# Four heads per tile, unnormalised weights and a ones column in the mixer of a two-block network

## The chip, the cores and the metric

The program runs on one core of a Trainium2 chip. The metric is device time in microseconds (us) of one execution; before the change three runs took 1721.58, 1722.12 and 1723.14 us, with a median of 1722.12. The core has a matrix engine (PE, with its weight loads as PEld), a vector engine (DVE), an activation engine (ACT), GpSimd (POOL) and a queue of loads (SP). Each works through its own list of instructions in order and waits on semaphores for the others.

## The reference, cut to what matters

Two blocks run one after the other on 256 tokens of width 1024. The second block has two layers, and each holds one mixer, the part that is changed. Cut to it:

```python
def hybrid_mixer(h, ...):
    z = h @ w_in
    q_lat, kv_lat, k_rope, qkv_d = jnp.split(z, [c0, c1, c2], axis=-1)
    q = (rmsnorm_2(q_lat, q_norm) @ w_q_up).reshape(B, S, 8, 64 + 32)
    kv = (rmsnorm_2(kv_lat, kv_norm) @ w_kv_up).reshape(B, S, 8, 64 + 64)
    ...
    o_mla = mla_attention(q_nope, q_rope, k_nope, k_rope, v_mla)   # 8 heads, causal
    qd, kd, vd = [t.reshape(B, S, 8, 64) for t in jnp.split(qkv_d, 3, axis=-1)]
    qd, kd = apply_rope(qd, cos_d, sin_d), apply_rope(kd, cos_d, sin_d)
    o_dil = dilated_attention(qd, kd, vd).reshape(B, S, 512)       # 8 heads, dilated windows
    merged = concatenate([rmsnorm_2(o_mla, gain[:512]), rmsnorm_2(o_dil, gain[512:])])
    return merged @ w_out

def apply_rope(x, cos, sin):
    x1, x2 = jnp.split(x, 2, axis=-1)
    return jnp.concatenate([x1 * cos - x2 * sin, x2 * cos + x1 * sin], axis=-1)
```

The kernel turns the three dilated windows into one masked softmax (the mask tile holds the logarithm of how often a key is seen), so both kinds of heads are a softmax of 256 queries over 256 keys, of which the first 128 queries see 128 keys.

## The kernel before, in words

Weights stream from memory in chunks of 16 blocks of 128x128. ACT copies half a chunk into a tile `whi` in a rounded format, DVE writes the rest, raw minus `whi`, into `wlo`, and PE multiplies with three matmuls a block (`whi` with both parts of the activations, `wlo` with one). These matmuls, called dense here, have 256 or 512 moving columns. The softmax parts use plain fp32, where one matmul leaves two records in the trace.

A recording layer (`Recorder`, L374) takes all operations of the program, gives each a due time, and puts each engine's list in the order of a modelled start (`order`, L472). PE takes what can start first, so softmax matmuls stand between dense ones that come later in the source. PSUM has eight tiles called `bank`; scratch tiles are called `n`, small columns `sm`, and the tiles of one stage `part`.

The mixer (L1634) streams these stages: `vd` (values of the dilated heads), `za` and `zb` (six tiles of 128 columns of z each), `kn`, `vm` and `q` (keys, values and queries of the other heads), and `o` (the product with w_out). Heads of the dilated kind (i = 1) start while `zb` streams, those of the other kind (i = 0) while `q` streams. `pipeline` (L1558) advances each live head by one step per new head.

- A tile of z has two heads of 64 rows. `rotate` (L1658) copies the four groups of 32 rows in swapped order with four ACT copies and then needs three DVE operations.
- One head's `attention` (L1449) is: a score matmul for the first 128 queries and one for the other 128; on DVE a masked minimum (a custom operation), on ACT the exponential with its sum as a second output; then on DVE a reciprocal and two divisions, on PE three transposes, on ACT a copy, and `weighted` (L1477) multiplies values, held as weights of 64 columns, with the transposed softmax.

```python
            nc.scalar.activation(s[:, a], s[:, a], AF.Exp, scale=-1.0, bias=m[:, t:t + 1], accum_out=den[:, t:t + 1])
        rd = self.small(2)
        nc.vector.reciprocal(rd, den)
        for t, a in enumerate((slice(0, P), slice(P, 384))):
            nc.vector.tensor_scalar(s[:, a], s[:, a], rd[:, t:t + 1], None, op0=OP.mult)
```

- Outputs have features on partitions, two heads in a bank. The norm of a kind (L1711 to L1723) squares on ACT, adds on DVE, sums over partitions on PE with `ones`, takes the power -0.5 on POOL, broadcasts with transposes of `sm` and multiplies on DVE.

In the trace nearly all of these operations carry one line, L667, where the recorded calls are made, so they are told apart by tiles.

## Time and profile before

| | |
|---|---|
| median of three runs | 1722.12 us |
| the profiled execution's own time | 1721.75 us |
| its span, first to last instruction | 1720.0 us |
| PE busy | 1669.3 us, 97% |
| DVE busy | 1198.2 us, 70% |
| ACT busy | 908.1 us, 53% |
| POOL busy | 59.5 us, 3% |

Matmuls are pipelined, so a record lasts longer than the time until the next one starts; what a matmul costs is read as the distance between starts. The first mixer lies at about 840 to 963 us, the second at about 1372 to 1494 us.

### The profile page before, as it was taken

Reading aid. Unit: us, or ns where it says so; the run is one execution under the profiler, and the core shown is the slowest. Engines: PE = TensorE matmul, PEld = TensorE weight load, DVE = VectorE, ACT = ScalarE, POOL = GpSimd, SP = SyncE. Lnnn points to the kernel's source line nnn. Section 1 sums busy time; section 2 is a strip of 40 time slices with the busy share of each in tenths; the row PEclk is TensorE's granted clock in tenths of the full one; section 3 lists DMA queues with packets and bytes.
Section 4 is the critical chain, followed back from the end, with each engine's and each line's share of the span. In section 5 each row is a group of like instructions: output and inputs, shape, how many; then the busy total and the mean of one; then the engine's idle time right before and its main releaser. Section 6 shows DMA issues by size and latency. Waiting matters only on the chain.

```text
span 1720.0 us, 22162 instructions
## 1 busy us (share of the span) xinstructions
PE 1669.3 (97%) x8452; PEld 1362.7 (79%) x8452; DVE 1198.2 (70%) x1992; ACT 908.1 (53%) x1451; POOL 59.5 (3%) x81
## 2 busy tenths in 40 slices
PE   7999999999999999999999999999999999999998
PEld 4777888879788887888887788887888887788886
DVE  4889999897786557664677756558665578766547
ACT  2784444446454435454577544456444468554435
POOL 0000000000000001000000100001000000000001
PEclk9999999999999999999999999999999999999999
DMA  8766999864375545554432545546455432364542
GB/s 337 262 253 269 344 349 350 327 229 188 135 296 178 189 172 212 186 195 178 181 132 74 189 174 194 183 173 217 177 193 185 158 148 99 128 233 178 190 171 86
DMA packets 49803, 348.81 MB, mean 203 GB/s; under 512 B 5765, under 2 KB 5901, under 8 KB 8480
## 3 DMA queue, kind: packets, MB, share of 16 engines
q1 hardware_dynamic: 46960, 338.73, 53.6%
q0 software_dynamic: 2304, 7.41, 1.3%
q8 instruction: 66, 1.08, 0.2%
q10 hardware_dynamic: 432, 1.26, 0.2%
q14 instruction: 41, 0.34, 0.1%
HBM read 346.31 MB, written 1.06 MB: 202 GB/s over the span
## 4 chain that ended last, share of the span: by engine, by line
PE 81%; DVE 9%; ACT 6%; issue 2%; DMA 1%; POOL 1%; POOLq 0%; ACTq 0%; DVEq 0%
PE bank L667 81%; DVE n L667 3%; ACT n L667 3%; DVE wlo L667 3%; ACT whi L667 2%; POOL sm L667 1%; DVE part L667 1%; DVE x L667 1%; DMA x<-in_x_dram 1%; ACT part L667 1%; DVE xhl L667 1%; DVE raw L667 0%; DMA raw<-in_wm_dram 0%; DVE sm L667 0%; ACT L667 0%
## 5 line engine op out<-in xcount | busy, mean ns | idle before, releaser
L667 DVE TENSOR_TENSOR wlo<-raw,whi 128x1024 fp32r<-128x1024 f32 (+1 forms) x575 | 651.0, 1144 | 372.4 <-ACT whi L667 371.1
L667 ACT ACTIVATE whi<-raw 128x1024 fp32r<-128x1024 f32 (+1 forms) x575 | 564.1, 993 | 504.0 <-PE bank L667 461.9
L667 PE MATMUL bank<-whi,xhl 128*128 128x512 f32 x2240 | 714.0, 395 | 6.3 <-ACT xhl L667 4.1
L667 PEld LDWEIGHTS bank<-whi,xhl 128*128 128x128 f32 x2240 | 419.3, 188 | 101.9 <-ACT xhl L667 9.2
L667 PE MATMUL bank<-whi,part 128*128 128x512 f32 x1464 | 462.8, 394 | 0.1
L667 PE MATMUL bank<-wlo,xhl 128*128 128x512 f32 x1120 | 439.5, 393 | 3.2 <-DVE wlo L667 2.7
L667 PEld LDWEIGHTS bank<-whi,part 128*128 128x128 f32 x1464 | 273.4, 188 | 59.1 <-DVE part L667 1.8
L667 PE MATMUL bank<-wlo,part 128*128 128x512 f32 x732 | 286.0, 391 | 0.0
L667 PEld LDWEIGHTS bank<-wlo,xhl 128*128 128x128 f32 x1120 | 210.6, 188 | 49.9 <-DVE wlo L667 8.2
L667 PEld LDWEIGHTS bank<-wlo,part 128*128 128x128 f32 x732 | 137.6, 188 | 29.0 <-issue 1.2
L667 PE MATMUL bank<-xhl,whi 128*128 128x256 f32 x768 | 146.9, 290 | 1.7 <-ACT xhl L667 1.6
L667 PEld LDWEIGHTS bank<-xhl,whi 128*128 128x128 f32 x768 | 121.6, 193 | 12.7 <-issue 6.7
L667 ACT ACTIVATE n<-bank 32x256 f32<-32x256 f32 (+3 forms) x172 | 80.2, 468 | 92.4 <-PE bank L667 85.9
L667 PE MATMUL bank<-xhl,wlo 128*128 128x256 f32 x384 | 109.3, 288 | 2.0 <-ACT part L667 2.0
L667 PE MATMUL bank<-ident,n 128*128 128x128 f32 x480 | 80.8, 278 | 14.2 <-DVE n L667 10.1
L667 POOL TENSOR_TENSOR sm<-sm,mhalf 128x1 f32<-128x1 f32 (+2 forms) x48 | 43.2, 904 | 1459.2 <-DVE sm L667 1386.0
L667 PEld LDWEIGHTS bank<-ident,n 128*128 128x128 f32 x480 | 59.0, 142 | 37.3 <-DVE n L667 12.2
L667 ACT ACTIVATE part<-bank 128x512 fp32r<-128x512 f32 (+3 forms) x112 | 55.8, 505 | 46.0 <-PE bank L667 44.3
L667 PEld LDWEIGHTS bank<-xhl,wlo 128*128 128x128 f32 x384 | 73.8, 192 | 4.7 <-ACT part L667 2.6
L667 DVE TENSOR_TENSOR part<-bank,part 128x512 fp32r<-128x512 f32 (+3 forms) x122 | 65.7, 551 | 3.6 <-ACT n L667 2.6
L667 ACT ACTIVATE n<-x 128x512 f32<-128x512 f32 x52 | 32.5, 625 | 58.2 <-DVE x L667 52.5
L667 DVE CUSTOM_DVE_ANT_0 raw<-raw,macc 128x1024 f32<-128x1024 f32 x48 | 57.5, 1222 | 3.5 <-DMA raw<-in_wm_dram 3.4
(141 smaller groups left out, 1152.7 us busy)
## 6 DMA issues: line engine op xcount, KB each, us to landing
raw<-in_ws_dram SPq DMA_DIRECT2D x266, 1024.0 KB, 4.8
raw<-in_wm_dram SPq DMA_DIRECT2D x56, 1024.0 KB, 6.2
macc<-in_rows_dram POOLq DMA_DIRECT2D x10, 512.0 KB, 5.2
x<-in_x_dram ACTq DMA_DIRECT2D x2, 512.0 KB, 12.3
n<-scr POOLq DMA_DIRECT2D x8, 128.0 KB, 6.8
out_dram<-x SPq DMA_DIRECT2D x4, 256.0 KB
n<-in_pt_dram POOLq DMA_DIRECT2D x4, 128.0 KB, 4.4
masks<-in_masks_dram POOLq DMA_DIRECT2D x1, 256.0 KB, 5.0
```

Of the source, the lines that this page charges most:

```text
L667: getattr(getattr(rec.nc, name), method)(*[real(v) for v in args], **{k: real(v) for k, v in kw.items()})
```

## The change

Six places differ. The columns of z are put in another order, so that a tile holds the first or the second 32 dimensions of four heads; the rotation is then two products and a difference or sum per tile, without ACT copies. Scores of the dilated kind are computed for four heads at a time from 32-row slices of these tiles, in two halves that add up in PSUM. `attend` takes two heads at once; the exponential gives no sum and nothing is divided before the transposes. The values have 65 columns a head, the last of them ones, and are now the moving operand, with the transposed softmax as weights, so the output has queries on partitions and the sum of the softmax in its 65th column. A reciprocal and one product on DVE then divide. The norm of a kind works on tiles with tokens on partitions (square with a sum on ACT, power on POOL, one product on DVE) and turns them with four transposes each before `o`. Between two stages a head step is skipped where the stream yields None.

The diff, cut; removed lines of the mixer stand in the listing above.

```diff
 def z_cols(u):
-    if u < 2:
-        return span(u)
-    if u == 2:
+    if u in (4, 5):
+        return span(u - 4)
+    if u == 10:
         return slice(256, 384)
-    if u == 3:
+    if u == 11:
         return KR_COLS
-    u -= 4
-    base = C2 + (u % 2) * 512 + (u // 2) * P
-    return slice(base, base + P)
+    g, i = divmod(u, 6)
+    return np.concatenate([C2 + (i // 2) * 512 + h * 64 + (i % 2) * 32 + np.arange(32) for h in range(4 * g, 4 * g + 4)])
...
+    def attend(self, ps, v, bias, scale, om):
+        nc = self.nc
+        s = []
+        for p in ps:
+            e, m = self.wide(384), self.small(2)
+            for t, a in enumerate((slice(0, P), slice(P, 384))):
+                nc.vector.tensor_tensor_reduce(e[:, a], p[:, a], bias[t], -scale, 1e38, op0=OP.add, op1=OP.min,
+                                               accum_out=m[:, t:t + 1])
+                nc.scalar.activation(e[:, a], e[:, a], AF.Exp, scale=-1.0, bias=m[:, t:t + 1])
+            s.append(e)
+        self.pe += 0.7
+        yield
+        w = []
+        for e in s:
+            pt = self.bank()
+            for i in range(3):
+                nc.tensor.transpose(pt[:, i * P:(i + 1) * P], e[:, i * P:(i + 1) * P], self.ident)
+            w.append(self.wide(384))
+            nc.scalar.activation(w[-1], pt[:, :384], AF.Copy)
+        self.pe += 0.7
+        yield
+        po = self.bank()[:, :260].split(65)
+        first = None
+        for t, parts in enumerate(((0,), (1, 2))):
+            for i in range(2):
+                for j in parts:
+                    o = nc.tensor.matmul(po[:, 2 * t + i], w[i][:, j * P:(j + 1) * P], v(j // 2, i), start=(t + i == 0),
+                                         stop=(j == parts[-1]), skip_group_check=True, after=first)
+                    first = first or o
+        rd = self.small(4)[:, :, None]
+        nc.vector.reciprocal(rd, po[:, :, 64:])
+        nc.vector.tensor_mul(om.flat().split(64), po[:, :, :64], rd.to_broadcast([P, 4, 64]))
+        self.pe += 0.7
     def mixer(self, l, h):
         nc = self.nc
         self.epoch()
         tl = self.tl
         rope, qlh, qd, kd = tl([3, T]), tl([3, 2 * T], FR), tl([4, T]), tl([4, T])
...
+        vd, vm, ka, qa = tl([2, 8, 65]), tl([2, 8, 65]), tl([8, T]), tl([8, T])
+        kr, lt, lr, oh = tl([T]), tl([T]), tl([512]), Halved(tl([2, 2, D], FR))
         accq, acck = self.squares(2), self.squares(1)
...
+        low, om = {}, {}
         rcol = self.r
...
+        for v in (vd, vm):
+            for t in range(2):
+                nc.vector.memset(v[:, t, :, 64:], 1.0)
+        def ropes():
+            pb = self.bank()
+            for t in range(2):
+                nc.tensor.transpose(pb[:, t * P:(t + 1) * P], rcol[t].to_broadcast([P, P]), self.ident)
+            r = nc.slot("rb", [P, T], FT)
+            nc.scalar.activation(r, pb[:, :T], AF.Copy)
+            for i, t in enumerate((self.cos_d, self.sin_d, self.rot_m)):
+                nc.vector.tensor_mul(rope[:, i], t, r)
+            return r
+        def rotate(da, db, pa, pb):
+            for dst, x, y, op in ((da, pa, pb, OP.subtract), (db, pb, pa, OP.add)):
+                t = self.tmp()
+                nc.vector.tensor_mul(t, y, rope[:, 1])
+                nc.vector.tensor_mul(dst, x, rope[:, 0])
+                nc.vector.tensor_tensor(dst, dst, t, op=op)
         half = slice(64, P)
+        held = {}
         def z(u, ps):
...
+            if not held:
+                held["r"] = ropes()
+            if u == 11:
                 nc.vector.tensor_mul(kr[half], ps[half, :T], rope[half, 2])
                 sw = self.tmp()
...
+                for i, j in ((64, 96), (96, 64)):
                     nc.scalar.activation(sw[i:i + 32], kr[j:j + 32], AF.Copy)
                 nc.vector.tensor_add(kr[half], kr[half], sw[half])
                 nc.vector.tensor_copy(ka[half], kr[half, None, :].to_broadcast([64, 8, T]))
...
+                return
+            g, i = divmod(u, 6)
+            if i < 4:
+                if i % 2 == 0:
+                    held[i] = ps
+                else:
+                    dst = (qd, kd)[i // 2]
+                    rotate(dst[:, 2 * g], dst[:, 2 * g + 1], held[i - 1], ps)
+                return
+            n = 2 if g else i - 4
+            ql = self.tmp()
+            nc.vector.tensor_mul(ql, ps[:, :T], held["r"])
+            acck[1](0, ql) if n == 2 else accq[1](n, ql)
+            self.hilo_scaled(qlh[:, n], ql, self.vec("kvn", l) if n == 2 else self.vec("qn", 2 * l + n))
+            if n == 2:
+                low["c"], _ = self.rnorm([(accq[0], 1.0 / 256), (acck[0], 1.0 / 128)], lr)
+                nc.vector.tensor_mul(lt, self.rot_m, lr[:, :T])
+        left = {}
+        def scores(i, j):
             if i == 0:
...
+                out = []
+                for u in (2 * j, 2 * j + 1):
+                    ps = self.bank()
+                    nc.tensor.matmul(ps[:, :P], qa[:, u, :P], ka[:, u, :P], start=True, stop=True)
+                    nc.tensor.matmul(ps[:, P:384], qa[:, u, P:], ka[:, u], start=True, stop=True)
+                    out.append(ps)
+                return out
+            if j % 2 == 0:
+                four = [self.bank() for _ in range(4)]
+                last = {}
+                for a, n in ((slice(0, P), P), (slice(P, 384), T)):
+                    for part in range(2):
+                        for e, ps in enumerate(four):
+                            b = slice(32 * e, 32 * e + 32)
+                            q, k = qd[b, j + part], kd[b, j + part]
+                            last[e] = nc.tensor.matmul(ps[:, a], q[:, a.start:a.start + P], k[:, :n], start=(part == 0),
+                                                       stop=(part == 1), share=4, after=last.get(e))
+                left[0] = four[2:]
+                return four[:2]
+            return left.pop(0)
+        def heads(i, j):
+            v = vd if i else vm
+            b, sc = (self.masks[:, :T], 64 ** -0.5) if i else (self.masks[:, T:], 96 ** -0.5)
+            if j == 0:
+                om[i] = self.row().split(T).split_last(P)
+            yield from self.attend(scores(i, j), lambda s, e: v[:, s, 2 * j + e], (b[:, P:], b), sc, om[i][:, j])
+            if j == 3:
+                for t in range(2):
+                    o, ss, m, r = om[i][:, :, t], self.small(1), self.small(1), self.small(1)
+                    nc.scalar.activation(self.wide().split(P), o, AF.Square, accum_out=ss)
+                    nc.vector.tensor_scalar(m, ss, 1.0 / 512, EPS, op0=OP.mult, op1=OP.add)
+                    nc.gpsimd.tensor_tensor(r, m, self.mhalf[:, :1], op=OP.pow)
+                    y = self.wide()
+                    nc.vector.tensor_scalar(y.split(P), o, r, None, op0=OP.mult)
+                    self.later(3.0, lambda t=t, y=y: self.turned(t, y, [(oh, self.vec("go", l * 8, 8), None)], 4 * i),
+                               oh.mem, t, range(4 * i, 4 * i + 4))
         def q_up(u, ps):
             nc.vector.tensor_mul(qa[:, u], ps[:, :T], lt)
@@ -1730,30 +1792,29 @@
                 a = slice(64 * s, 64 * s + 64)
                 nc.vector.tensor_mul(ka[:64, 2 * u + s], ps[a, :T], lr[a, T:])
+        def values(dst, scale):
+            return lambda t, _, ps: nc.scalar.activation(dst[:, t, :, :64], ps.split(64), AF.Copy, scale=scale(t))
         def stream():
...
+            self.natural(f"b{l}vd", h, values(vd, lambda t: rcol[t]), tail=None)
             self.units(f"b{l}za", h, z)
             yield heads(1, 0)
...
             for u in self.steps(f"b{l}zb", h, lambda u, ps: z(u + 6, ps)):
...
+                yield {0: 1, 3: 2, 4: 3}.get(u) and heads(1, {0: 1, 3: 2, 4: 3}[u])
             ql = Tall(qlh)
             for _ in self.steps(f"b{l}kn", ql, k_up, lambda k, u: 2):
                 pass
...
+            yield None
+            self.natural(f"b{l}vm", ql, values(vm, lambda t: low["c"][:, 2 + t:3 + t]), at=lambda k: 2)
             for u in self.steps(f"b{l}q", ql, q_up):
...
+                if u % 2:
+                    yield heads(0, u // 2)
         self.pipeline(stream())
         grow = self.fixed_row(l * 4 + 1)
         hn = self.xhl()
         then = self.gained([(hn, self.gain(l, 4), None)])
...
+        self.natural(f"b{l}o", oh, self.add_normed(grow, 1.0 / D, then), halves=2, tail=self.TAIL,
                      at=lambda k: (k + 4) % 8)
         return hn
```

On PE, the first scores of the first mixer; `xhl` is the mixer's input, `part_3` and `part_2` hold keys and queries. Before:

```order
L667 MATMUL bank_135<-xhl_77,whi_69 128x256 x2
L667 MATMUL bank_129<-part_3_5985,part_2_5984 128x128
L667 MATMUL bank_129<-part_3_5985,part_2_5984 128x256
L667 MATMUL bank_133<-part_3_5985,part_2_5984 128x128
L667 MATMUL bank_133<-part_3_5985,part_2_5984 128x256
L667 MATMUL bank_135<-xhl_77,wlo_74 128x256
```

The same place now:

```order
L676 MATMUL bank_131<-part_3_5975,part_2_5974 128x128
L676 MATMUL bank_135<-xhl_77,whi_70 128x256
L676 MATMUL bank_135<-xhl_77,wlo_75 128x256
L676 MATMUL bank_135<-xhl_77,whi_70 128x256 x2
L676 MATMUL bank_136<-part_3_5975,part_2_5974 128x128
L676 MATMUL bank_129<-part_3_5975,part_2_5974 128x128
L676 MATMUL bank_133<-part_3_5975,part_2_5974 128x128
L676 MATMUL bank_131<-part_3_5975,part_2_5974 128x128
L676 MATMUL bank_136<-part_3_5975,part_2_5974 128x256
```

Four matmuls on four banks stand alone, four dense ones follow, and then come the second halves of the first queries and all eight matmuls of the other queries.

On PE, after the last of these scores, where `n` holds the softmax and `part_4` the values. Now:

```order
L676 MATMUL bank_131<-part_3_5975,part_2_5974 128x256
L676 MATMUL bank_135<-xhl_77,wlo_75 128x256
L676 MATMUL bank_135<-xhl_77,whi_70 128x256 x2
L676 MATMUL bank_135<-xhl_77,wlo_75 128x256
L676 MATMUL bank_134<-ident,n_120 128x128
L676 MATMUL bank_135<-xhl_77,whi_70 128x256
L676 MATMUL bank_132<-ident,n_110 128x128
L676 MATMUL bank_135<-xhl_77,whi_70 128x256
L676 MATMUL bank_135<-xhl_77,wlo_75 128x256
L676 MATMUL bank_134<-ident,n_120 128x128 x2
```

The first transpose stands four dense matmuls behind the scores; before, 20 dense matmuls stood between the last score of a head pair and its first transpose.

On PE, values times softmax of the first two heads. Before:

```order
L667 MATMUL bank_131<-xhl_77,wlo_76 128x256
L667 MATMUL bank_132<-n_117,part_4_5986 64x256
L667 MATMUL bank_132<-n_117,part_4_5986 64x128
L667 MATMUL bank_131<-xhl_77,whi_71 128x256 x2
L667 MATMUL bank_131<-xhl_77,wlo_76 128x256
L667 MATMUL bank_136<-ident,n_110 128x128
```

Now:

```order
L676 MATMUL bank_135<-xhl_77,wlo_75 128x256
L676 MATMUL bank_136<-part_4_5976,n_115 128x65
L676 MATMUL bank_136<-part_4_5976,n_111 128x65
L676 MATMUL bank_136<-part_4_5976,n_115 128x65 x2
L676 MATMUL bank_136<-part_4_5976,n_111 128x65 x2
L676 MATMUL bank_129<-ident,n_113 128x128 x3
L676 MATMUL bank_133<-ident,n_117 128x128 x3
```

Two matmuls a head became three, two heads stand together, and the transposes of the next two heads follow at once.

## Rows read from the trace of the kernel before

**Rows 1.** The page's first part: busy us, share of the span and instructions.

```profile
span 1720.0 us, 22162 instructions
PE 1669.3 (97%) x8452; PEld 1362.7 (79%) x8452; DVE 1198.2 (70%) x1992; ACT 908.1 (53%) x1451; POOL 59.5 (3%) x81
```

**Rows 2.** Windows, softmax parts: us, busy PE, PEld, DVE, ACT, POOL; clock, DMA.

```profile
865.00:947.00 82.00, 76.80 (x511) 62.79 (x509) 62.22 (x202) 61.89 (x164) 3.52 (x3) 0.98 0.27 98
1397.00:1479.00 82.00, 77.14 (x512) 61.95 (x511) 63.02 (x204) 61.62 (x165) 3.29 (x3) 1.00 0.27 96
```

**Rows 3.** Waits of PE in 865 to 947: us in total, times, longest.

```profile
PE bank L667 <- DVE n L667: 2.8, 4, 1.1
PE bank L667 <- ACT n L667: 1.3, 3, 0.6
PE bank L667 <- POOL sm L667: 0.7, 1, 0.7
```

**Rows 4.** Timeline of PE, one head's values times softmax: start, us, form, records.

```profile
884.25 0.28 PE L667 MATMUL bank<-xhl,wlo 128*128 128x256 f32 x1
884.52 0.86 PE L667 MATMUL bank<-n,part 128*64 128x256 f32 x4
885.31 0.51 PE L667 MATMUL bank<-xhl,whi 128*128 128x256 f32 x2
885.65 0.29 PE L667 MATMUL bank<-xhl,wlo 128*128 128x256 f32 x1
```

**Rows 5.** Groups of PE in 865 to 947: records | busy us, mean ns.

```profile
L667 PE MATMUL bank<-ident,n 128*128 128x128 f32 x48 | 10.6, 283 | 3.0 <-DVE n L667 2.8
L667 PE MATMUL bank<-ones,acc 128*128 128x1 f32 x28 | 3.9, 247 | 0.3 <-DVE sm L667 0.3
```

**Rows 6.** Timeline of PE, sums of one kind's norm.

```profile
943.41 0.39 PE L667 MATMUL bank<-whi,part 128*128 128x512 f32 x1
943.64 0.95 PE L667 MATMUL bank<-ones,acc 128*128 128x1 f32 x8
944.44 0.49 PE L667 MATMUL bank<-whi,part 128*128 128x512 f32 x1
944.77 0.40 PE L667 MATMUL bank<-wlo,part 128*128 128x512 f32 x1
```

**Rows 7.** Timeline of PE, scores of two dilated heads.

```profile
889.65 0.40 PE L667 MATMUL bank<-xhl,whi 128*128 128x256 f32 x2
889.98 0.93 PE L667 MATMUL bank<-part,part 64*128 64x128 f32 x8
890.84 0.38 PE L667 MATMUL bank<-xhl,wlo 128*128 128x256 f32 x1
891.06 0.40 PE L667 MATMUL bank<-xhl,whi 128*128 128x256 f32 x2
891.30 0.28 PE L667 MATMUL bank<-xhl,wlo 128*128 128x256 f32 x1
```

**Rows 8.** Timeline of PE, four 32-column slices of an early product.

```profile
10.07 1.94 PE L667 MATMUL bank<-raw,cs 128*32 128x512 f32 x8 [1.06 <-DMA raw<-in_wm_dram]
```

**Rows 9.** Groups of DVE in 865 to 947.

```profile
L667 DVE CUSTOM_DVE_ANT_0 n<-bank,masks 128x256 f32<-128x256 f32 x16 | 6.6, 416 | 1.6 <-PE bank L667 1.6
L667 DVE TENSOR_SCALAR n<-n,sm 128x256 f32<-128x256 f32 x16 | 5.6, 348 | 0.0
L667 DVE TENSOR_SCALAR n<-n,sm 128x128 f32<-128x128 f32 x16 | 4.5, 280 | 0.0
```

**Rows 10.** Groups of ACT in 865 to 947.

```profile
L667 ACT ACTIVATE n<-bank 32x256 f32<-32x256 f32 x32 | 12.0, 375 | 2.4 <-DVE part L667 2.0
L667 ACT ACTIVATE n<-n,sm 128x256 f32<-128x256 f32 x16 | 8.0, 501 | 1.4 <-DVE sm L667 1.3
L667 ACT ACTIVATION_READ_ACCUMULATOR n<-n,sm 128x1 f32 x32 | 6.0, 187 | 0.0
```

**Rows 11.** Window of PE in the first mixer; PEclk is third from the end.

```profile
875.00:878.00 3.00, 3.00 (x15) 2.92 (x14) 2.40 (x7) 2.58 (x6) 0.00 (x0) 0.50 0.00 0
```

More of the change, by code (lines that the diff above doesn't have):

```diff
@@ L220, in const_cols @@
     c[:, 0] = inv64[p % 32]
-    c[:, 1] = np.where(p % 64 < 32, -1.0, 1.0)
+    c[:, 1] = 1.0
     c[:, 2] = np.where(p >= 64, inv32[p % 16], 0.0)
@@ L314, in split, with split_last @@
                     self.chain + [("split", n)])
+    def split_last(self, n):
+        d0, (size, st) = self.dims
+        return View(self.mem, self.base, [d0, (size // n, st * n), (n, st)], self.off, self.part, self.dtype,
+                    self.chain + [("split_last", n)])
     def flat(self):
@@ L337, in real @@
                 a = a.rearrange("p (a b) -> p a b", b=x)
+            elif kind == "split_last":
+                a = a.rearrange("p a (b c) -> p a b c", c=x)
             elif kind == "flat":
@@ L1561, in pipeline @@
         for g in gens:
-            live.append(g)
+            if g is not None:
+                live.append(g)
             live = [x for x in live if next(x, self) is not self]
@@ L1645, in mixer @@
         rcol = self.r
-        got = []
-        def r():
-            if not got:
-                pb = self.bank()
-                for t in range(2):
-                    nc.tensor.transpose(pb[:, t * P:(t + 1) * P], rcol[t].to_broadcast([P, P]), self.ident)
-                got.append(nc.slot("rb", [P, T], FT))
-                nc.scalar.activation(got[0], pb[:, :T], AF.Copy)
-            return got[0]
-        def rotate(dst, ps):
-            sw = self.tmp()
-            for i, j in quads:
-                nc.scalar.activation(sw[i:i + 32], ps[j:j + 32, :T], AF.Copy)
-            nc.vector.tensor_mul(sw, sw, rope[:, 1])
-            nc.vector.tensor_mul(dst, ps[:, :T], rope[:, 0])
-            nc.vector.tensor_add(dst, dst, sw)
@@ L1667, in mixer @@
-        quads = ((0, 32), (32, 0), (64, 96), (96, 64))
+        for v in (vd, vm):
[10 more added lines that the diff above has]
+            return r
@@ L1684, in z @@
+            if u == 11:
                 nc.vector.tensor_mul(kr[half], ps[half, :T], rope[half, 2])
                 sw = self.tmp()
-                for i, j in quads[2:]:
+                for i, j in ((64, 96), (96, 64)):
                     nc.scalar.activation(sw[i:i + 32], kr[j:j + 32], AF.Copy)
@@ L1689, in z @@
                 nc.vector.tensor_copy(ka[half], kr[half, None, :].to_broadcast([64, 8, T]))
-            else:
-                dst = (qd, kd)[u % 2][:, (u - 4) // 2]
-                rotate(dst, ps)
-        ops, even = {}, {}
-        def heads(i, u):
-            if i == 0:
-                q, k, v, b, sc = qa[:, u], ka[:, u], vm, self.masks[:, T:], 96 ** -0.5
-            else:
-                a = slice((u % 2) * 64, (u % 2) * 64 + 64)
-                q, k, v, b, sc = qd[a, u // 2], kd[a, u // 2], vd, self.masks[:, :T], 64 ** -0.5
-            def o(v, w):
-                if u % 2 == 0:
-                    even[i] = v, w
-                else:
-                    ops[i] = self.bank()
-                    self.weighted((ops[i][:64, :T], *even.pop(i)), (ops[i][64:, :T], v, w))
-            yield from self.attention(q, k, lambda s: v[:, s, u * 64:(u + 1) * 64], (b[:, P:], b), sc, o)
-            if u % 2:
-                t = u // 2
-                nc.scalar.activation(om[i][:, t], ops[i][:, :T], AF.Copy)
-                if t == 0:
-                    acco[i] = self.squares(4)
-                acco[i][1](t, om[i][:, t])
-                if t == 3:
-                    ro = self.rnorm([(acco[i][0], 1.0 / 512)], copy=False)[1]
-                    for j in range(4):
-                        y = self.tmp()
-                        nc.vector.scalar_tensor_tensor(y, om[i][:, j], self.vec("go", l * 8 + i * 4 + j), ro,
-                                                       op0=OP.mult, op1=OP.mult)
-                        self.hilo(oh[:, i * 4 + j], y)
@@ L1755, in mixer @@
         then = self.gained([(hn, self.gain(l, 4), None)])
-        self.natural(f"b{l}o", Tall(oh), self.add_normed(grow, 1.0 / D, then), halves=2, tail=self.TAIL,
+        self.natural(f"b{l}o", oh, self.add_normed(grow, 1.0 / D, then), halves=2, tail=self.TAIL,
                      at=lambda k: (k + 4) % 8)
```

28 lines of the change are left out of this document (removed).

## The prediction, made before the changed kernel was run

> **What bounds the kernel.** I read the page's busy shares first: PE is busy for 97% of the span, DVE for 70%, ACT for 53% [rows 1]. PE sets the time, so an edit is worth what it takes off PE's own list, plus what it takes off PE's waits. Then I cut the span into windows. Two stretches of 82 us, one in each layer's mixer, hold the softmax work. PE idles 82 - 76.80 = 5.2 us in the first and 82 - 77.14 = 4.9 us in the second, 10.1 us in all; DVE and ACT are busy for some 62 of the 82 us, so neither is full, but both are close enough to be late at times [rows 2]. The waits of PE in the first stretch are on DVE's softmax tiles (2.8 us in 4 waits) and ACT's (1.3 us in 3) more than on POOL [rows 3]. At best, then, the waits are worth 10 us of 1722, and the rest must come out of matmuls.
>
> What a matmul costs I take from starts in the timeline. Dense ones of 256 columns follow each other at 0.12 us (two between 891.06 and 891.30, [rows 7]), those of 512 at 0.23 us (943.41 to 943.64, [rows 6]). For a visit of other matmuls between dense ones I take the distance from the dense start ahead of it to a dense start behind it, less the dense pitches in between. The shorter dense rows right behind a visit start late, so part of the price of a visit sits there.
>
> **Values times softmax.** One head before: from 884.25 to 885.65 are 1.40 us, with three dense pitches in them, so the visit costs 1.04 us [rows 4]. A layer has 16 heads; by this row they cost 16.6 us, and as some heads share a visit I take 16.0. Now two heads stand together: three matmuls a head, two records each, so 12 records with 65 moving columns and 128 columns of weights. The nearest row with 128 columns of weights and few moving ones is the sum with `ones`: eight records cost 943.41 to 944.77 less two pitches of 0.23, 0.90 us, or 0.11 each, with one moving column [rows 6]. Twelve cost 1.35, eight visits 10.8 us. That is 5.2 us less a layer. From below: the four records of [rows 4] stream 2 x 256 + 2 x 128 = 768 columns in 0.79 us, 1.03 ns a column, so 65 columns alone would be 0.067, a visit 0.8 with 0.1 for entry, 7 us a layer, 9 less. From above, a record costs as much as one there, 0.20, which is 19 us a layer, 3 more. I take 0.11, because the load of 128 weight columns is the same and the streaming is shorter than it.
>
> Here the two differ from a rule: the Trainium skill, "TensorEngine Tiling", section "Instruction Overhead", says that a matmul with one moving column lasts as long as one with 60, some 60 cycles, which counts moving columns alone. The row puts the one-column record at 0.11 us, more than 65 streamed columns need. By the rule the lower end would hold, and the time would be near 1699 us; by the row it is the value taken, and the measurement decides.
>
> **Scores of the dilated kind.** Before, four visits a layer of two heads: 889.65 to 891.06 less three pitches is 1.05 us, together 4.2 [rows 7]. The pair streams eight records of 1536 columns, 1.58 us at 1.03 ns if one after the other, so the two 64-row halves do run side by side. Now a visit has four heads in 32-row slices, and each score is a sum of two matmuls, so it streams twice as long as a pair for twice as many heads: 2.1 us for four if all four run side by side, nothing won. The nearest row for four slices is an early product in four 32-column slices: eight records of 512 columns would be 4.2 us in line and end within 1.94 [rows 8]. As the first four matmuls stand alone in the list, with four dense ones behind them, I add an entry, 0.15 us a visit: 0.3 us more a layer. If the slices do not overlap, eight half scores cost 0.79 each [rows 4], 6.3 us for four heads, 8.4 more a layer. Below I see no gain over 0.5.
>
> **Norms and transposes.** The 48 softmax transposes of a layer [rows 5] stay 48. Of the 28 records with `ones` in a stretch [rows 5] 16 belong to the output norms and go, 1.8 us, with four broadcasts of `sm`, 0.4; 16 transposes of the outputs come, 1.8 at 0.11. That is 0.4 us less a layer. The scores of the other kind and all dense matmuls stay.
>
> **DVE and ACT.** In a layer DVE loses two divisions a head, 5.6 + 4.5 us [rows 9], and a reciprocal; it gains a reciprocal and a product a pair. ACT loses the 32 copies of the rotation, 12.0 us, and the 32 reads of sums, 6.0 [rows 10]. None of this counts by itself, since neither engine sets the end. It counts where PE waits: between an exponential and its transposes a reciprocal, two divisions (0.28 and 0.35) and two reads of 0.19 go. Against this the cover shrinks: 20 dense matmuls stood between the first scores and their first transpose, now four, 0.48 us. I take half of the idle time off, 2.5 us a layer; the bounds are 5 less and 5 more.
>
> **The sum.** A layer: -5.2 + 0.3 - 0.4 - 2.5 = -7.8 us; two layers -15.6. The profiled execution took 1721.75 us (span 1720.0 and 1.75 around it), 0.4 under the median of the three runs. 1721.75 - 15.6 + 0.4 = 1706.5 us; I say 1706.
>
> **Rivals.**
> - *The idle time stays.* The first four heads need cos, sin and 12 operations on DVE before the second half scores can go, at most 0.42 us each (the length of a 256-column operation in [rows 9]), 5.9 us, while PE has 40 dense matmuls, 4.8 us, and the four scores take four of eight banks. A wait of 1 us for each of the four groups of the two layers and some at pairs would bring the 10.1 us back. Time: 1721.75 - 10.6 = 1711. For it: DVE is close to full [rows 2]. Against it: the chain behind the scores is shorter by five operations.
> - The Trainium skill, "TensorEngine Tiling", section "Gotcha 1: PSUM Pressure", says that row tiles raise the pressure on PSUM because each writes to a bank of its own. No wait in [rows 3] is on a bank, so the trace is silent on it; by the rule the case above would be likelier, with its time.
> - *Idle goes altogether*, as the chains end in time, and the weights load a little quicker: 1721.75 - 10.6 - 10.1 = 1701.
> - *The 32-row slices do not overlap.* 8.4 instead of 0.3 us a layer, 16.2 more in all: 1722.7, no change. For it: no row has 32-row slices. Against it: two 64-row ones and four 32-column ones overlap.
> - *The pairs leave PE uncovered, and it gets slower.* A pair's transposes need four reductions (0.42 at most) and a last exponential (0.50): 2.2 us, less 0.48 of dense cover, 1.7 us for each of 16 pairs: 27 us in place of 10.1, 1721.75 - 10.6 - 10.1 + 27 = 1728. It turns slower once the mean wait of a pair passes (10.1 + 10.6) / 16 = 1.3 us. Against it: the first reductions start while PE still computes the scores of the other queries, and most later pairs have the values of an earlier pair (1.35 us) and 12 dense matmuls between.
>
> The granted clock fell to 0.50 from 875 to 878 us, the lower of its two levels (1.2 GHz), behind a stretch of sums, broadcasts and a wait [rows 11]. Such a stretch of 3 us costs 1.5. Whether it stays, goes or comes twice I can't tell; it is inside the range.
>
> **Chances.** The forecast 0.50, with a range of its own from 1702 to 1710; idle stays 0.20; idle goes 0.15; no overlap 0.08; slower pairs 0.07. The measurement can't tell less than 0.2%, 3.4 us, from no change. Faster is 0.50 + 0.20 + 0.15 = 0.85, the same 0.08, slower 0.07. The range from 1696 to 1717 holds the first three but for a part of the quickest; it leaves out some 0.2.
>
> **What would show it.** Records of values times softmax about 0.11 us apart, twelve in a row, then dense ones at once. Sixteen scores of a group in 2.1 to 2.3 us with starts of four close together. PE's idle in the two stretches between 2 and 3 us each. Wrong it would be if these twelve records cost near 2.4 us, if the four slices start one after the other, or if PE waits for ACT's exponentials ahead of most pairs' transposes.

## The result, and the profile after

The changed kernel takes 1701.52 us (median of 4 runs, 1701.12 to 1702.02) against 1721.85 us of the kernel before on the same chip, a ratio of 0.988 with a 95% interval from 0.9868 to 0.9892: 20.3 us less. Forecast were 15.6 us less.

The page's first part, as in [rows 1]:

```profile
span 1699.3 us, 22230 instructions
PE 1655.5 (97%) x8572; PEld 1368.7 (81%) x8572; DVE 1185.2 (70%) x1924; ACT 870.1 (51%) x1299; POOL 60.2 (4%) x85
```

PE has 120 records more and is busy 13.8 us less. To see where, each mixer is cut from the same instruction to the same instruction: from the eight transposes of `x` ahead of it to those of the next stage. The columns are those of [rows 2]. Before:

```profile
845.08:959.39 114.31, 108.39 (x690) 90.00 (x690) 83.61 (x239) 78.68 (x195) 5.15 (x6) 0.99 0.33 119
1376.74:1490.29 113.55, 107.99 (x690) 88.72 (x690) 84.18 (x239) 78.53 (x197) 4.92 (x6) 1.00 0.33 120
```

After:

```profile
844.95:948.78 103.83, 101.75 (x750) 92.24 (x750) 77.48 (x205) 59.71 (x121) 6.22 (x9) 1.00 0.37 136
1365.91:1469.69 103.78, 101.68 (x750) 92.25 (x750) 77.47 (x205) 59.72 (x121) 6.21 (x9) 1.00 0.37 136
```

The mixers are shorter by 10.48 and 9.77 us, together 20.25, so all of the gain lies here. Length less busy is PE's idle time: 5.92 and 5.56 us before, 2.08 and 2.10 now. In the second mixer busy time falls by 6.31 us and idle time by 3.46. The first gives 0.7 us more. It had the 3 us at half clock [rows 11]: up to there the two mixers before run alike to 0.01 us, and at its end, at 877.8 us, the first is 1.3 us behind. From there on PE's order differs between them, so not all of the 0.7 can be put down to the clock. Now the mean clock is 1.00 in both.

PE's waits in the first mixer, as in [rows 3]; the first row is one wait of 1.0 us ahead of the first scores of the other kind and one of 0.37 among the dilated scores; the rows left out have 0.5 and 0.2 us, both before 850 us. None is ahead of a softmax transpose any more:

```profile
PE bank L676 <- DVE sm L676: 1.4, 2, 1.0
...
```

Values times softmax in PE's timeline (start, us, form, records), where [rows 4] stood, once with the next transposes behind it and once alone:

```profile
881.02 0.28 PE L676 MATMUL bank<-xhl,wlo 128*128 128x256 f32 x1
881.14 1.45 PE L676 MATMUL bank<-part,n 128*128 128x65 f32 x12
882.43 0.83 PE L676 MATMUL bank<-ident,n 128*128 128x128 f32 x6
883.01 0.48 PE L676 MATMUL bank<-xhl,whi 128*128 128x256 f32 x2
883.33 0.28 PE L676 MATMUL bank<-xhl,wlo 128*128 128x256 f32 x1
...
885.85 0.28 PE L676 MATMUL bank<-xhl,wlo 128*128 128x256 f32 x1
885.97 1.45 PE L676 MATMUL bank<-part,n 128*128 128x65 f32 x12
887.23 0.48 PE L676 MATMUL bank<-xhl,whi 128*128 128x256 f32 x2
887.55 0.28 PE L676 MATMUL bank<-xhl,wlo 128*128 128x256 f32 x1
```

Alone, two heads cost 887.55 - 885.85 less three dense pitches of 0.12, 1.34 us. With six transposes the visit costs 1.95, so these add 0.61, 0.10 each. The twelve records take 1.29 us up to the start of the first transpose, 0.107 each.

The scores of the first four heads, where [rows 7] stood:

```profile
874.44 0.28 PE L676 MATMUL bank<-xhl,whi 128*128 128x256 f32 x1
874.65 0.50 PE L676 MATMUL bank<-part,part 32*128 32x128 f32 x8
875.09 0.39 PE L676 MATMUL bank<-xhl,whi 128*128 128x256 f32 x1
875.31 0.28 PE L676 MATMUL bank<-xhl,wlo 128*128 128x256 f32 x1
875.43 0.39 PE L676 MATMUL bank<-xhl,whi 128*128 128x256 f32 x2
875.75 0.94 PE L676 MATMUL bank<-part,part 32*128 32x128 f32 x16
877.06 1.12 PE L676 MATMUL bank<-part,part 32*128 32x256 f32 x8 [0.37 <-DVE sm L676]
878.12 0.39 PE L676 MATMUL bank<-xhl,wlo 128*128 128x256 f32 x1
878.34 0.40 PE L676 MATMUL bank<-xhl,whi 128*128 128x256 f32 x2
```

Eight records end within 0.50 us; their 8 x 128 columns in line would take 1.05 at the prediction's 1.03 ns a column, so the four slices overlap. From 874.44 to 878.34 less six pitches are 3.18 us, 0.37 of it a wait. A layer's second group has no wait:

```profile
891.26 0.40 PE L676 MATMUL bank<-xhl,whi 128*128 128x256 f32 x2
891.59 0.50 PE L676 MATMUL bank<-part,part 32*128 32x128 f32 x8
892.03 0.38 PE L676 MATMUL bank<-xhl,wlo 128*128 128x256 f32 x1
892.34 1.37 PE L676 MATMUL bank<-part,part 32*128 32x128 f32 x24
893.64 0.50 PE L676 MATMUL bank<-xhl,whi 128*128 128x256 f32 x2
893.98 0.28 PE L676 MATMUL bank<-xhl,wlo 128*128 128x256 f32 x1
```

That is 2.72 less five pitches, 2.12 us.

### The profile page after: what moved, and what is told of

Its sections match the earlier page's. It is cut to its first block, busy times and chain, and to the rows that moved or that the text cites. A ratio compares the mean times of both kernels' runs of the same rounds, so it can differ in the third digit from the quotient of the medians.

```text
span 1699.3 us, 22230 instructions
## 1 busy us (share of the span) xinstructions
PE 1655.5 (97%) x8572; PEld 1368.7 (81%) x8572; DVE 1185.2 (70%) x1924; ACT 870.1 (51%) x1299; POOL 60.2 (4%) x85
## 3 DMA queue, kind: packets, MB, share of 16 engines
HBM read 346.31 MB, written 1.06 MB: 204 GB/s over the span
## 4 chain that ended last, share of the span: by engine, by line
PE 83%; DVE 10%; ACT 3%; issue 2%; DMA 1%; POOL 1%; POOLq 0%; ACTq 0%; DVEq 0%
PE bank L676 83%; DVE n L676 3%; DVE wlo L676 3%; DVE part L676 1%; ACT whi L676 1%; ACT n L676 1%; POOL sm L676 1%; DVE x L676 1%; DMA x<-in_x_dram 1%; DVE xhl L676 1%; ACT part L676 1%; DMA raw<-in_wm_dram 0%; DVE raw L676 0%; DVE macc L676 0%; DVE sm L676 0%
## 5 line engine op out<-in xcount | busy, mean ns | idle before, releaser
L676 ACT ACTIVATE n<-bank 128x512 f32<-128x512 f32 (+2 forms) x108 | 54.9, 522 | 83.6 <-PE bank L676 82.3
L676 POOL TENSOR_TENSOR sm<-sm,mhalf 128x1 f32<-128x1 f32 (+1 forms) x52 | 44.0, 849 | 1438.2 <-DVE sm L676 1438.0
L676 ACT ACTIVATE part<-bank 128x512 fp32r<-128x512 f32 (+3 forms) x96 | 49.7, 525 | 38.2 <-PE bank L676 36.6
```

The lines of the kernel that those rows point to most:

```text
L676: getattr(getattr(rec.nc, name), method)(*[real(v) for v in args], **{k: real(v) for k, v in kw.items()})
```

## The experiments

Ahead of the first mixer all kernels are the same, and yet in the profiles it starts anywhere from 844.3 to 847.5 us. So besides the median the length of the mixer is given. The changed kernel, run a second time as a yardstick, took 1702.50 us (1701.88 to 1703.51), 1.0 more than the first time, while its second mixer, at 103.77 us, repeated to 0.01.

> The changed kernel itself, unaltered, as the yardstick for the three others of this set on the same chip: 1701.5 us as before, within 0.5 us.

All kernels, with the second mixer in us (idle is length less busy). Each ratio is to the kernel before on the same chip, where its median was 1721.85 to 1722.53 us. The mean clock of the second mixer was 0.97 with the copies back and 0.93 with the copies beside, and 1.00 in all others, so those two lengths and busy times hold a lower clock as well:

| kernel | median | ratio to before, interval | length, PE busy, idle |
|---|---|---|---|
| before | 1721.85 | | 113.55, 107.99, 5.56 |
| changed | 1701.52 | 0.988 (0.9868 to 0.9892) | 103.78, 101.68, 2.10 |
| new z and scores alone | 1716.92 | 0.9968 (0.9955 to 0.998) | 111.20, 108.30, 2.90 |
| new heads and outputs alone | 1708.11 | 0.9916 (0.9903 to 0.993) | 106.66, 101.51, 5.15 |
| divisions back | 1704.81 | 0.9898 (0.9884 to 0.9911) | 105.33, 102.66, 2.67 |
| copies back | 1711.09 | 0.9929 (0.9916 to 0.9941) | 109.60, 105.05, 4.55 |
| copies beside, shared scratch | 1728.06 | 1.0029 (1.0018 to 1.004) | 115.91, 109.94, 5.97 |
| copies as load | 1707.34 | 0.9914 (0.99 to 0.9927) | 106.13, 102.92, 3.21 |
| one head at a time | 1705.14 | 0.9901 (0.9887 to 0.9915) | 105.42, 103.16, 2.26 |
| 120 columns | 1701.95 | 0.9884 (0.9871 to 0.9897) | 103.51, 101.46, 2.05 |
| halves | 1700.46 | 0.9875 (0.9861 to 0.989) | 103.57, 101.88, 1.69 |
| halves, copy on ACT | 1701.28 | 0.988 (0.9868 to 0.9893) | 103.64, 101.86, 1.78 |
| halves, later heads | 1701.81 | 0.9882 (0.9869 to 0.9896) | 103.84, 102.25, 1.59 |

**The two halves of the change.** First without the new z: old columns, rotation with copies, scores of two heads.

```diff
-                rotate(dst[:, 2 * g], dst[:, 2 * g + 1], held[i - 1], ps)
+                rotate((qd, kd)[u % 2][:, (u - 4) // 2], ps)
...
-                        for e, ps in enumerate(four):
-                            b = slice(32 * e, 32 * e + 32)
+                for e, ps in enumerate(two):
+                    b = slice(64 * e, 64 * e + 64)
```

> The changed kernel with one part undone: the old order of the columns of z, the rotation with 32 ACT copies a layer, and the scores of the dilated kind for two heads at a time from 64-row slices. Values, outputs and norms stay as changed. Theory A (the waits of PE went because the chain from scores to transposes lost two divisions, a reciprocal and two reads of sums): PE's idle time stays at about 1.8 us a layer, and the scores cost 4.2 us a layer again in place of the 5.1 and 5.1 seen in the changed kernel, so some 1.5 us less: 1700 us. Rival B (the waits went because the copies left ACT and the rotation's chain): the 3.5 us of idle a layer come back, 7 us in all: 1707 us, with PE's waits on ACT's copies and DVE's rotation ahead of the scores.

It took 1708.11 us. Its second mixer, and PE's longest waits in the first:

```profile
1370.45:1477.11 106.66, 101.51 (x719) 91.78 (x719) 77.76 (x205) 72.74 (x153) 7.04 (x9) 1.00 0.37 133
```

```profile
PE bank L675 <- DVE part L675: 3.2, 4, 1.0
...
```

Busy time is that of the changed kernel, 101.51 against 101.68, so the scores of four save nothing on PE. The idle time is nearly all back, and `part` is what DVE's rotation writes: PE waits for it ahead of each of the four score visits. Theory A falls for the idle time, rival B stands.

Then the other half alone, with the old heads, values and norms; a head takes its bank from the scores of four:

```diff
-                q, k, v, b, sc = qd[a, u // 2], kd[a, u // 2], vd, self.masks[:, :T], 64 ** -0.5
+                q, k, v, b, sc = None, None, vd, self.masks[:, :T], 64 ** -0.5
+                if u % 4 == 0:
+                    four = [self.bank() for _ in range(4)]
...
+                    left[0] = four
+                q = left[0].pop(0)
```

> The other half of the change alone: the kernel before with the new order of z, the rotation without copies and the scores of four heads, but with the old chain a head (sums, reciprocal, divisions), values as weights, and the old norms. Undoing this half in the changed kernel cost 6.6 us. Theory A (the two halves add up): 6 to 7 us less than before, 1715 to 1716 us. Rival G (the old chain leaves PE uncovered when four heads' scores come at once): 1718 us or more, with longer waits of the transposes on DVE. Rival H (either half takes the same waits away): under 1713 us.

```profile
1374.28:1485.48 111.20, 108.30 (x722) 89.53 (x722) 82.85 (x239) 67.33 (x165) 5.31 (x6) 1.00 0.34 122
```

1716.92 us is 0.9 above theory A's range, and yet the halves nearly add up: by the medians to 5.6 + 14.1 = 19.7 of 20.3 us, in the second mixer to 2.35 + 6.89 = 9.24 of 9.77. And they split cleanly. The new z takes 2.66 us of idle and adds 0.3 busy; the new heads and outputs take 6.48 busy and 0.4 idle. A long chain a head with four heads' scores at once did not uncover PE. PE's longest waits in the first mixer:

```profile
PE bank L668 <- DVE part L668: 0.8, 2, 0.5
...
```

The waits on softmax tiles (`n`) that led [rows 3] are gone here although the divisions are back, and they are gone without the new z as well, where the waits for the rotation have come in their place.

**The chain a head.** The sums, reciprocal and divisions put back into the changed kernel:

```diff
-                nc.scalar.activation(e[:, a], e[:, a], AF.Exp, scale=-1.0, bias=m[:, t:t + 1])
+                nc.scalar.activation(e[:, a], e[:, a], AF.Exp, scale=-1.0, bias=m[:, t:t + 1], accum_out=den[:, t:t + 1])
+            nc.vector.reciprocal(rs, den)
+            for t, a in enumerate((slice(0, P), slice(P, 384))):
+                nc.vector.tensor_scalar(e[:, a], e[:, a], rs[:, t:t + 1], None, op0=OP.mult)
```

> The changed kernel with the sums of the exponentials, a reciprocal a head and the two divisions a head put back ahead of the transposes; the ones column then sums to one and everything else stays. It adds 32 divisions (10.1 us of DVE) and 32 reads of sums (6 us of ACT) a layer. Theory A (a shorter chain took the waits away): most of the 3.5 us of idle a layer come back, 1705 to 1708 us, as waits of PE's transposes on DVE. Rival B (the rotation's copies were what PE waited for): 1701 to 1703 us, idle of PE within 1 us a layer of the changed kernel's.

```profile
1366.99:1472.32 105.33, 102.66 (x750) 92.16 (x750) 84.92 (x253) 63.00 (x153) 6.30 (x9) 1.00 0.37 134
```

1704.81 us, between the two. Of 1.55 us more a layer only 0.57 are idle; 0.98 are busy time with the same 750 records, and no wait stands ahead of a transpose. Most of it lies in the scores of the second group, which have no wait in the changed kernel and here have that of the first group (second mixer):

```profile
1413.51 0.28 PE L676 MATMUL bank<-xhl,wlo 128*128 128x256 f32 x1
...
1415.78 1.12 PE L676 MATMUL bank<-part,part 32*128 32x256 f32 x8 [0.37 <-DVE sm L676]
...
1417.05 0.28 PE L676 MATMUL bank<-xhl,wlo 128*128 128x256 f32 x1
```

From 1413.51 to 1417.05 less three pitches are 3.18 us against 2.12: 1.06 of the 1.55. Counted in the timeline, the small work stands in 34 separate visits between dense matmuls, against 25 in the changed kernel and 41 before; for these nine visits more, 0.3 us of busy time is left. The run puts 10 us on DVE and 6 on ACT besides the longer chain, and does not tell load and chain apart.

**The copies.** Put back into the rotation of the changed kernel:

```diff
+                for i in range(0, P, 32):
+                    nc.scalar.activation(t[i:i + 32], y[i:i + 32, :T], AF.Copy)
-                nc.vector.tensor_mul(t, y, rope[:, 1])
+                nc.vector.tensor_mul(t, t, rope[:, 1])
```

> The changed kernel with 32 ACT copies of 32 rows a layer put back ahead of the rotation's products, where the kernel before had them, so that ACT does 12 us more a layer and the rotation's chain is longer by them; the order of z and all matmuls stay. Theory A: PE's idle grows by under 1 us a layer, 1702 to 1703 us. Rival B: 3.5 us of idle a layer come back, 1707 to 1709 us.

Its first mixer, undisturbed by the clock, and PE's longest waits from 870 to 903 us:

```profile
847.05:953.77 106.72, 102.17 (x751) 92.51 (x751) 78.23 (x205) 72.37 (x153) 6.23 (x9) 1.00 0.36 133
```

```profile
PE bank L676 <- DVE part L676: 1.9, 3, 0.9
...
```

2.9 us more than the changed kernel's, 2.5 of it idle, ahead of the scores. The second mixer lost 2.9 us more to the clock (below). The median is 1711.09, above rival B's range; the two of the five runs with the shortest times took 1707.06 and 1708.39. Rival B stands.

Is it the chain or ACT's load? The first try had the same copies write a tile that nothing reads:

```diff
+                    nc.scalar.activation(unread[i:i + 32], y[i:i + 32, :T], AF.Copy)
```

> The changed kernel with the same 32 ACT copies of 32 rows a layer as in the run that put them back, at the same place, but written to a tile that nothing reads, so that the rotation doesn't wait for them. Theory F (they cost because they stand in the chain from z to the scores): 1702 to 1704 us, and PE's idle time ahead of the scores stays at that of the changed kernel. Rival L (they cost because ACT has 12 us more to do a layer and is late with everything else): 1706 to 1709 us, as with the copies in the chain.

It came out slower than before, 1728.06 us, and tells nothing on the question: the unread tile is one of the scratch tiles `n` that go round, so DVE waited for the copies all the same (one row of its waits from 870 to 903 us):

```profile
...
DVE n L676 <- ACT n L676: 1.3, 2, 0.8
...
```

The second try has a tile of its own, and reads the rotated tiles after the rotation, so that the scores wait for nothing more:

```diff
+                for i in range(0, P, 32):
+                    held["spare"] = nc.scalar.activation(spare[:32], dst[i:i + 32, :240], AF.Copy)
```

> The changed kernel with 32 further ACT copies of 32 rows a layer (240 columns each) which read the rotated tiles after the rotation and write a tile that nothing reads; they have until the first outputs, and DVE and PE wait for none of them until then. Theory F (the rotation's copies cost by standing in the chain from z to the scores): 1701.5 to 1703 us, no new wait of PE ahead of scores. Rival L (they cost as load on ACT): 1705 to 1709 us, PE's waits on exponentials and halves of weights grow by 2 us a layer or more.

1707.34 us; one visit of values times softmax in the first mixer:

```profile
888.01 0.38 PE L676 MATMUL bank<-part,n 128*128 128x65 f32 x2
888.76 1.33 PE L676 MATMUL bank<-part,n 128*128 128x65 f32 x10 [0.36 <-ACT n L676]
```

2.35 us a layer more, with no copy in the chain: rival L's time, with only part of the waits that it named. The row's wait is not ahead of scores but within the values, where the second head's transposed softmax comes late from ACT. Idle time grows by 1.1 us; the rest of the 2.35 shows as busy time. A wait shorter than a record lasts would show so, but that is argued, not measured. So 12 us more of ACT cost PE 2.4 us here and 2.9 in the rotation, though ACT is busy for only 69% of this mixer (58% of the changed kernel's); the place decides who waits. Other places were not tried.

**Visits.** One head at a time, `attend` being called for a head instead of a pair, with the same records:

```diff
-        for e in s:
-            pt = self.bank()
+        pt = self.bank()
...
-                yield {0: 1, 3: 2, 4: 3}.get(u) and heads(1, {0: 1, 3: 2, 4: 3}[u])
+                j = {0: 2, 3: 4, 4: 6}.get(u)
+                yield j and heads(1, j)
+                yield j and heads(1, j + 1)
```

> The changed kernel with heads taken one at a time: transposes in visits of three and values times softmax in visits of six records; instructions and their sizes stay the same. Theory A (a visit of PE away from the dense matmuls has a price of its own, and the transposes fell from 0.41 us for three in two visits to 0.61 us for six in one): 1.7 us a layer for transposes and 0.5 to 1 for values come back, 1705 to 1707 us. Rival C (only records count, 0.11 us each, however they are grouped): 1701 to 1702.5 us.

Transposes of one head in PE's timeline:

```profile
896.11 0.40 PE L676 MATMUL bank<-xhl,whi 128*128 128x256 f32 x2
896.47 0.44 PE L676 MATMUL bank<-ident,n 128*128 128x128 f32 x2
896.66 0.36 PE L676 MATMUL bank<-xhl,wlo 128*128 128x256 f32 x1
896.87 0.27 PE L676 MATMUL bank<-ident,n 128*128 128x128 f32 x1
896.89 0.48 PE L676 MATMUL bank<-xhl,whi 128*128 128x256 f32 x2
897.21 0.28 PE L676 MATMUL bank<-xhl,wlo 128*128 128x256 f32 x1
```

1705.14 us, in theory A's range, with 1.64 us a layer of the 2.2 to 2.7 that it named. Idle hardly changes; 1.48 us of busy time come with 37 visits in place of 25, 0.12 each on average. Both kinds pay: three transposes in two visits cost 897.21 - 896.11 less five pitches, 0.50 us, where three behind values cost 0.30; six records of values alone cost 0.62 to 0.95 in the seven such visits of the second mixer, where half a pair alone costs 0.67 to 0.75. But a visit has no fixed price: in the changed kernel the first six transposes of the second mixer stand in four visits (dense starts at 1399.56 and 1401.06, seven pitches between) and cost 0.66 us, against 0.61 for six in one.

**Moving columns.** Values times softmax with 120 columns:

```diff
-        vd, vm, ka, qa = tl([2, 8, 65]), tl([2, 8, 65]), tl([8, T]), tl([8, T])
+        vd, vm, ka, qa = tl([2, 575]), tl([2, 575]), tl([8, T]), tl([8, T])
...
-            yield from self.attend(scores(i, j), lambda s, e: v[:, s, 2 * j + e], (b[:, P:], b), sc, om[i][:, j])
+            yield from self.attend(scores(i, j), lambda s, e: v[:, s, (2 * j + e) * 65:(2 * j + e) * 65 + 120], (b[:, P:], b), sc, om[i][:, j])
```

> The changed kernel with 120 moving columns a head instead of 65 in values times softmax (the 55 more are the next heads' values, whose products nothing reads); weights, counts and the order of instructions stay. Theory A (a record with 128 columns of weights has a price of its own, 0.107 us, under which the moving columns hide): twelve records still take 1.29 us, and the time stays within 1 us of the changed kernel. Rival D (the moving columns set it, at the 1.03 ns a column read before, from a floor below 0.107 us): a record rises by up to 0.057 us, 96 records a layer by 5.4 us, 1704 to 1712 us.

```profile
887.18 0.28 PE L676 MATMUL bank<-xhl,wlo 128*128 128x256 f32 x1
887.30 1.50 PE L676 MATMUL bank<-part,n 128*128 128x120 f32 x12
888.56 0.48 PE L676 MATMUL bank<-xhl,whi 128*128 128x256 f32 x2
888.88 0.28 PE L676 MATMUL bank<-xhl,wlo 128*128 128x256 f32 x1
```

888.88 - 887.18 less three pitches is 1.34 us, as with 65: theory A. The columns are free here. The Trainium skill, "TensorEngine Tiling (Array Packing)", section "Instruction Overhead", has such a floor, and says that it reaches to 60 columns. In these plain fp32 products with 128 columns of weights it reaches to 120 at least, at 0.107 us a record. Fewer columns of weights were not tried, so that the weights set this floor is not shown.

**Attempts at a better version.** In the first group's scores the last four matmuls wait for DVE's first reduction in the same bank (the 0.37 us above). So the loop was turned round, first halves of both query blocks, then second halves, and each of these matmuls was ordered behind the one before it (that part isn't shown):

```diff
-                for a, n in ((slice(0, P), P), (slice(P, 384), T)):
-                    for part in range(2):
+                for part in range(2):
+                    for a, n in ((slice(0, P), P), (slice(P, 384), T)):
```

> The changed kernel with the score matmuls of four heads in another order: first half for both query blocks, then second half for both, in place of both halves of the first block and then of the second. In the changed kernel the last four matmuls of the first group start one by one, 0.1 to 0.2 us apart, each behind DVE's reduction of the first block in the same bank, and the two visits cost 2.8 us against 2.3 in the second group. Theory W (they wait for DVE's reading of the bank): the first group falls by 0.4 to 0.9 us a layer, 1700 to 1701 us. Rival: the rotation of the second half or PE's order sets it, no change, 1701.5 us.

The second group in PE's timeline:

```profile
...
891.45 1.59 PE L676 MATMUL bank<-part,part 32*128 32x128 f32 x32
...
```

The wait is gone, as theory W has it, and the second group costs 1.71 us in place of 2.12 (dense starts at 891.12 and 893.19, less three pitches), but the planner broke the first group into four visits of 3.3 us together, against 2.81 and the wait of 0.37, so 0.2 us a layer remain of the 0.4 expected at least. Whether the chip needs that wait or only the program's semaphores ask for it, no run tells. At 1700.46 us it has the lowest median of all; its interval overlaps that of the changed kernel, and only the length of the mixer, which repeats, tells them apart.

Two more edits on top of it aimed at the wait of 1.0 us ahead of the first scores of the other kind. First the copy of the rotated key part on ACT:

```diff
-                nc.vector.tensor_copy(ka[half], kr[half, None, :].to_broadcast([64, 8, T]))
+                nc.scalar.activation(ka[half], kr[half, None, :].to_broadcast([64, 8, T]), AF.Copy)
```

> The last kernel, and besides the copy of the rotated key part to eight heads (64x2048, 1.2 us of DVE) moved to ACT. In the changed kernel PE waits 0.98 us a layer ahead of the first scores of the other kind while DVE works through eight key products, this copy and two outputs without a pause. Theory: DVE's backlog ends a microsecond sooner, and the wait falls by 0.5 to 0.98 us a layer: 1 to 2 us below the last kernel, 1698.5 to 1700 us. Rival: ACT, which then has 1.8 us more to do there, is late with the next halves of weights, and the time stays or rises by up to 2 us.

1701.28 us, and PE's wait there is still 0.9 us: nothing was gained. DVE, freed of the copy, now works off half a chunk of `wlo` (1.22 us at 908.09) ahead of the query product behind which PE starts; in the changed kernel it stood behind that product (at 909.55). So the run doesn't tell what the copy alone is worth.

Then, without that, later heads:

```diff
-                if u % 2:
-                    yield heads(0, u // 2)
+                if u in (2, 4, 6, 7):
+                    yield heads(0, {2: 0, 4: 1, 6: 2, 7: 3}[u])
```

> The kernel with the score matmuls in the order of halves, and besides the heads of the other kind started one unit of the q stage later (behind units 2, 4, 6 and 7 in place of 1, 3, 5 and 7), so that 6 more dense matmuls stand ahead of their first scores. Theory: the wait of 0.98 us a layer ahead of them (DVE's key products take 0.42 us each there) is covered by the 0.7 us of dense matmuls, 1699 to 1700 us. Rival: the last heads then crowd at the end of the stage with less between them, and 0.5 to 2 us come back as waits or clock: 1701 to 1703 us.

The wait fell to 0.5 us, another of 0.4 came behind it, and the mixer is 0.27 us longer than without this edit, with 0.10 less idle and 0.37 more busy: what the theory promised did not come, and 1701.81 us lies in the rival's range, with a loss at its lower end.

## Why the prediction was right, and where it was not

1701.52 us lies in the range from 1696 to 1717 and on the right side, but just below the forecast's own range, which began at 1702 (the second run of the same kernel, at 1702.50, just inside it). By the second mixer a layer gave 9.8 us instead of 7.8: busy time 6.3 instead of 5.3, idle time 3.5 instead of 2.5.

- **What bounds it** held: PE's own list gave the larger part, its waits the rest, and no other part of the program changed.
- **Values times softmax** held to the hundredth: 1.34 us a visit for 1.35, 0.107 us a record for 0.11. That the moving columns don't set the price is shown by the run with 120; that the 128 columns of weights do, the prediction's reason, stays argued.
- **Scores** were mis-sized: +0.3 us a layer was forecast against 4.2 before. The second group's 2.12 us fit the 2.25 forecast for each; the first costs 2.81 and 0.37 of waiting, as DVE reads a bank that PE has still to write, which the sum left out. That makes +0.7 and a wait. The overlap of the slices, which a rival denied, is there.
- **Transposes**: "The 48 softmax transposes of a layer [rows 5] stay 48" failed as a price. The records stayed, their price did not: three in two visits cost 0.41 us on average in the kernel before, six behind the values 0.61 now. For 48 that is 6.6 against 4.9 us a layer, a part of which the price of the values held already. Of this size is what the sum lacked: busy time fell by 1.0 us more than forecast, although the scores were 0.4 dearer. Fewer visits are the likely reason, 25 in place of 41 in the second mixer, but not one that is shown to the end: one head at a time costs 0.12 for each further visit, the divisions put back about 0.03. What the norms alone gave (0.4 forecast) was not measured apart.
- **Idle time**: 2.5 us a layer was near the 3.5, but for the wrong reason, and that it came near is luck. The step that failed is "between an exponential and its transposes a reciprocal, two divisions (0.28 and 0.35) and two reads of 0.19 go". With that shorter chain and the old rotation 5.15 us of idle remain, now as waits for the rotation; with the old chain and the new rotation 2.90. It was the 32 ACT copies, 12.0 us [rows 10], which the prediction counted at nothing by themselves: in the rotation they held the scores back, and as mere load they hold back what ACT does next. The chain has a price too, 1.55 us a layer when put back, 1.06 of it in the second group's scores and none as a wait ahead of a transpose. The sign to look for, 2 to 3 us of idle in each of the two stretches, was missed on the good side: 1.4 us are left there.
- **Less cover** for the transposes cost nothing: no wait stands ahead of one. The rival of slower pairs falls with it, and so does the one in which the idle time stays.
- **Idle goes altogether** forecast 1701, the time that came, but by another sum: 10.1 us of waits and 10.6 of matmuls there, against 7.3 and 13.0 in the two mixers.
- **The clock** was left open. Its 3 us at 0.50 are gone from the first mixer. They had put it 1.3 us behind the second, near the 1.5 named, and are part of the 0.7 us between the two gains.

## What to carry to other kernels

Count visits between streams of dense matmuls as well as records, but measure them: twelve more cost 0.12 us each in one run, nine more about 0.03 in another. An engine that is busy 69% of a stretch can still hold up the one that bounds it, so load taken off it is worth testing as load and as a link of the chain, one run each. When a change has two parts, run each alone: busy and idle time of the bounding engine then say which part did what.

## What was not expected of the hardware

A wait of PE can cost more behind it than itself. In the run with copies beside, PE was idle for 1.6 us of the first stretch and 1.8 of the third; behind each it ran at the lower of its two clock levels, for 6 and 13 us (PEclk third from the end):

```profile
876.00:881.00 5.00, 3.40 (x35) 2.65 (x37) 3.18 (x9) 4.33 (x13) 0.00 (x0) 1.00 0.00 0
882.00:888.00 6.00, 6.00 (x30) 5.35 (x31) 3.77 (x19) 3.17 (x9) 0.00 (x0) 0.50 0.01 3
899.00:902.00 3.00, 1.22 (x16) 0.89 (x14) 2.56 (x7) 2.25 (x6) 0.00 (x0) 1.00 0.49 156
902.00:915.00 13.00, 12.63 (x72) 11.03 (x69) 6.28 (x24) 6.37 (x16) 1.12 (x1) 0.50 0.34 127
```

This is why that mixer takes 117 us with only 3.7 us more of idle than the changed kernel's. With the copies back in the rotation the granted clock was 0.54 from 1425 to 1432 us in the second mixer, behind waits of 0.69 and 0.37 us; in its first mixer the same two waits were followed by full clock, as is the wait of 1.0 us in the changed kernel.
